# An unused 64-byte tile ahead of layer 0's pools in a two-layer hybrid attention / recurrence kernel

## The chip, the cores and the metric

The kernel runs on one core of one Trainium2 chip. The metric is the device time of one execution in microseconds; the median of several executions counts.

## The reference

The reference runs two layers over 1024 latent tokens and 256 context tokens of width 1024, in float32. Layer 0 projects the normalised tokens with one large matrix (9232 columns) into the parts of two mixers, 16 heads of neighbourhood attention and 4 heads of a bidirectional mLSTM, and projects their gated outputs back:

```python
qa, ka, va, za, qb, kb, vb, ob, zb, g = _split_cols(h @ w_in, AB_SIZES)
...
oa_l = _neighbourhood_attention(qa_l, ka_l, va_l, ka_c, va_c, rpb)
hb_l, hb_c = _mlstm_bidir(mb_l, mb_c, need_ctx)
...
return jnp.concatenate([ya, yb], axis=-1) @ w_out
```

Layer 1 has 16 heads of a bidirectional gated recurrence (HGRN2) between an input and an output projection of the same kind. Each layer's result is added to the stream with a gate per column.

## The kernel before

**Products.** TensorE takes float32 here in a rounded form, so each projection is made of three matmuls: an operand x is split into a rounded part (h) and the rest (l), and `dense` (lines 128 to 134) adds h times h, h times l and l times h for each of eight blocks of 128 rows:

```python
for k in range(nk):
    mm(ps, lhsT=lh(k), rhs=rh(k), start=(start and k == 0), stop=False, skip_group_check=skip)
    mm(ps, lhsT=lh(k), rhs=rl(k), start=False, stop=False, skip_group_check=skip)
    m = mm(ps, lhsT=ll(k), rhs=rh(k), start=False, stop=(stop and k == nk - 1), skip_group_check=skip)
```

These are the profile's lines L131, L132 and L133. `lhsT` is the stationary operand, which a weight load (PEld in the profile) brings into the array, and `rhs` the moving one, which streams through. The profile's rows name the moving operand first: `mm<-wh,hh` has the weights moving and the tokens stationary, `mm<-hh,wh` the other way round.

**The forms of layer 0.** `hh` and `hl` hold the split, normalised tokens (128 partitions, 8 blocks of 1280 tokens). `proj_nat` has 256 or 512 weight columns moving against 128 stationary tokens: 256 in `na_qk`, `na_values` and `proj_out`, 512 in `proj_wide`. `proj_tr` has 512 tokens moving (256 for the context) against 128 stationary weight columns, in `na_z` and `proj_out_tr`. The output projection (`out_sum`, lines L923 to L925) has 512 columns of the output weights moving against 128 stationary tokens of the mixers' result (`yh`, `yl`). Its weights lie in tiles `woh`, `wol`; six of eight blocks of its first half, `wh` and `wl`, still lie in layer 0's ring.

**Weights.** `wblock` (lines 81 to 121) fetches 128 x 512 weights by DMA into `wraw`, splits them on ScalarE and VectorE into `wh` and `wl`, and takes these tiles from a ring of six (`self.slabs`) in the pool `w0`.

**Stages of layer 0.** First the modulation, the normalisation and the first values (pool `pre`), then the gates of the mLSTM beside two more projections (pools `graw` and `gates`), then the attention of eight pairs of heads, with the next pair's projections and parts of the mLSTM's woven in (pool `na`), then the mLSTM's recurrence with the remaining projections woven in as filler (pool `ml`), then the output projection. A scheduler orders the instructions of each engine when the kernel is built.

**Where tiles lie.** Tiles are cut from each partition's bytes by pools that are stacked from the left, or, with `side="right"`, from the right end. On the left come the constants (pool `const`), then `mlk` (tables that the mLSTM keeps), `w0`, and above them in turn `graw`, `pre`, `gates`, `na` and `ml`. On the right lie `edge` (32 bytes), `hh` and `hl`, and later the output projection's tiles. At the end of layer 0 its pools are closed, and those of layer 1 begin again right behind `const`. The lines are these:

```python
edge = es.enter_context(tc.tile_pool(name="edge", bufs=1, side="right"))
...
self.open_h(right)
l0 = es.enter_context(ExitStack())
mlk = l0.enter_context(tc.tile_pool(name="mlk", bufs=1))
self.wp = l0.enter_context(tc.tile_pool(name="w0", bufs=2))
```

Of the kernel before, what the change touches and what calls it, by code (L numbers as in the profile page):

```python
# [10 lines left out]
F32 = mybir.dt.float32  # L11
# [8 lines left out]
P = 128  # L20
# [25 lines left out]
class Prog:  # L46
# [1520 lines left out]
    def build(self):  # L1567
        tc, nc, a = self.tc, self.nc, self.a
        dma = nc.sync.dma_start
        with ExitStack() as es:  # L1570
# [71 lines left out]
            self.open_h(right)  # L1642
            l0 = es.enter_context(ExitStack())
            mlk = l0.enter_context(tc.tile_pool(name="mlk", bufs=1))
            self.wp = l0.enter_context(tc.tile_pool(name="w0", bufs=2))
            self.rawp = self.wp
            self.slabs = 6
# [621 lines left out]
```

## Time and profile before

| | before |
|---|---|
| median of 3 runs | 3318.89 us (3318.3 to 3319.4) |
| the profiled execution | 3318.67 us |
| its span, first to last instruction | 3316.9 us |
| DMA queues | 286,032 packets, 236.73 MB by SyncE's; 51,760 packets, 138.94 MB by GpSimd's |
| granted TensorE clock | 9 or more tenths in all 40 slices |

How to read it: the page divides the span by engine, then by lines. A group's row gives line, engine, operation, tiles, shape and count, then the busy time of the group, the mean duration of one in ns, and the idle time ahead of it. The timeline gives start and duration in us of each instruction. A matmul's duration runs over its passage through the array, and several are under way at a time; how fast they follow each other is read from the spacing of their starts.

### The profile page before, as it was taken

What the parts mean: (1) busy time and instruction counts of PE and PEld (TensorE: products, weight loads), DVE (VectorE), ACT (ScalarE), POOL (GpSimd) and SP (SyncE); (2) the same over time, 40 slices, a digit from 0 to 9 for tenths busy, and PEclk for the clock granted to TensorE, in tenths of its full rate; (3) what the DMA queues carried; (4) which work ended last, traced back from release to release, by engine and by line L of the source; (5) the groups of instructions that cost most, each with busy time, mean ns of one, the idle gap of its engine ahead of it and who ended that gap; (6) DMA issues with size and microseconds to landing.
All of it is one profiled execution on the core that took longest, in us unless ns stands there. A gap on an engine that the chain in (4) does not pass through costs nothing.

```text
span 3316.9 us, 64819 instructions
## 1 busy us (share of the span) xinstructions
PE 3268.9 (99%) x24814; PEld 2905.1 (88%) x24814; DVE 2173.8 (66%) x4978; ACT 1455.9 (44%) x3396; POOL 796.5 (24%) x1191
## 2 busy tenths in 40 slices
PE   7999999999999999999999999999999999999999
PEld 6699899988989888898888788899999999999977
DVE  5337666666655566687767755577677677677756
ACT  5335554455544444455446333333433433433443
POOL 2222222222211112221110233312333333333110
PEclk9999999999999999999999999999999999999999
DMA  7713222232233433444653333322322324334376
GB/s 246 247 52 84 85 71 82 69 94 84 72 87 105 145 113 123 131 141 144 210 179 100 100 102 105 104 74 76 120 76 93 117 79 112 95 85 107 91 213 165
DMA packets 338102, 379.82 MB, mean 115 GB/s; under 512 B 34600, under 2 KB 269800, under 8 KB 336768
## 3 DMA queue, kind: packets, MB, share of 16 engines
q1 hardware_dynamic: 286032, 236.73, 24.2%
q0 software_dynamic: 51760, 138.94, 13.3%
q8 instruction: 196, 3.21, 0.4%
q14 instruction: 114, 0.93, 0.1%
HBM read 272.31 MB, written 103.08 MB: 113 GB/s over the span
## 4 chain that ended last, share of the span: by engine, by line
PE 80%; DVE 7%; issue 5%; DMA 4%; ACT 2%; POOL 1%; SPq 1%; DVEq 0%; POOLq 0%; ACTq 0%
PE mm L131 15%; PE mm L132 14%; PE mm L133 14%; PE acc L861 2%; PE s L1401 2%; PE tr L841 2%; PE mm L923 2%; PE mm L925 2%; PE mm L924 2%; PE x L131 2%; PE x L133 2%; PE x L132 2%; PE acc L633 2%; PE s L642 2%; PE s L1472 1%
## 5 line engine op out<-in xcount | busy, mean ns | idle before, releaser
L131 PE MATMUL mm<-wh,hh 128*128 128x256 f32 (+1 forms) x1440 | 446.2, 310 | 2.2 <-DVE graw L1694 0.8
L132 PE MATMUL mm<-wl,hh 128*128 128x256 f32 (+1 forms) x1440 | 444.9, 309 | 0.0
L133 PE MATMUL mm<-wh,hl 128*128 128x256 f32 (+1 forms) x1440 | 442.2, 307 | 0.0
L131 PE MATMUL mm<-hh,wh 128*128 128x512 f32 (+1 forms) x1076 | 392.0, 364 | 1.0 <-ACT p L1211 0.7
L132 PE MATMUL mm<-hl,wh 128*128 128x512 f32 (+1 forms) x1076 | 387.6, 360 | 0.7 <-DVE hl L318 0.7
L133 PE MATMUL mm<-hh,wl 128*128 128x512 f32 (+1 forms) x1076 | 387.4, 360 | 0.0
L131 PE MATMUL mm<-wzh,hh 128*128 128x256 f32 x1024 | 296.4, 289 | 0.0
L131 PEld LDWEIGHTS mm<-wh,hh 128*128 128x128 f32 x1440 | 271.6, 189 | 21.1 <-ACT ev L352 3.4
L132 PE MATMUL mm<-wzl,hh 128*128 128x256 f32 x1024 | 286.2, 280 | 0.0
L133 PE MATMUL mm<-wzh,hl 128*128 128x256 f32 x1024 | 285.6, 279 | 0.0
L132 PEld LDWEIGHTS mm<-wl,hh 128*128 128x128 f32 x1440 | 271.6, 189 | 12.3 <-issue 0.7
L133 PEld LDWEIGHTS mm<-wh,hl 128*128 128x128 f32 x1440 | 271.4, 189 | 12.0 <-issue 0.5
L131 PEld LDWEIGHTS mm<-hh,wh 128*128 128x128 f32 x1076 | 202.9, 189 | 33.5 <-ACT ev L371 4.2
L133 PEld LDWEIGHTS mm<-hh,wl 128*128 128x128 f32 x1076 | 202.6, 188 | 29.7 <-issue 0.2
L132 PEld LDWEIGHTS mm<-hl,wh 128*128 128x128 f32 x1076 | 202.9, 189 | 28.6 <-DVE hl L318 1.4
L131 PEld LDWEIGHTS mm<-wzh,hh 128*128 128x128 f32 x1024 | 192.8, 188 | 2.4
L132 PEld LDWEIGHTS mm<-wzl,hh 128*128 128x128 f32 x1024 | 192.7, 188 | 0.0
L133 PEld LDWEIGHTS mm<-wzh,hl 128*128 128x128 f32 x1024 | 192.0, 188 | 0.0
L74 DVE TENSOR_TENSOR wl<-wraw,wh 128x512 fp32r<-128x512 f32 x174 | 118.6, 689 | 85.6 <-ACT wh L73 83.8
L1436 ACT COPY gksel<-gK 128x1024 f32<-128x1024 f32 x96 | 110.9, 1155 | 100.1 <-DVE gK L1431 43.7
L1431 DVE TENSOR_TENSOR gQ<-gQ,gF 128x1024 f32<-128x1024 f32 x112 | 140.4, 1253 | 20.4 <-PE s L1401 20.4
L1431 DVE TENSOR_TENSOR gK<-gK,gF 128x1024 f32<-128x1024 f32 x112 | 140.2, 1251 | 18.8 <-ACT gksel L1436 11.4
(598 smaller groups left out, 8523.8 us busy)
## 6 DMA issues: line engine op xcount, KB each, us to landing
wraw<-in_wab_dram SPq DMA_DIRECT2D x108, 256.0 KB
wraw<-yd SPq DMA_DIRECT2D x92, 256.0 KB
br<-in_wc_dram SPq DMA_DIRECT2D x66, 256.0 KB
md<-ev POOLq DMA_DIRECT2D x60, 256.0 KB, 2.6
wraw<-in_wc_dram SPq DMA_DIRECT2D x120, 128.0 KB
mloz<-md SPq DMA_DIRECT2D x40, 256.0 KB
s<-gyt POOLq DMA_DIRECT2D x36, 256.0 KB, 5.7
adar<-in_wada_dram SPq DMA_DIRECT2D x16, 512.0 KB
```

The lines of the kernel that those rows point to most:

```text
L74: nc.vector.tensor_tensor(out=lo, in0=x, in1=hi.bitcast(F32), op=ALU.subtract)
L131: mm(ps, lhsT=lh(k), rhs=rh(k), start=(start and k == 0), stop=False, skip_group_check=skip)
L132: mm(ps, lhsT=lh(k), rhs=rl(k), start=False, stop=False, skip_group_check=skip)
L133: m = mm(ps, lhsT=ll(k), rhs=rh(k), start=False, stop=(stop and k == nk - 1), skip_group_check=skip)
L633: nc.tensor.matmul(num, lhsT=qc[:, j, :], rhs=C[d][:, j, :], start=False, stop=(j == 1))
L642: nc.tensor.matmul(u, lhsT=st["k"][c][:, j * P : (j + 1) * P], rhs=vw, start=True, stop=True)
L841: nc.tensor.transpose(pt[:nk, i, :], pr[:, o : o + nk], self.ident)
L861: m = nc.tensor.matmul(yp[h64], lhsT=v[:, h64], rhs=pTs[hd][:nk, i, :], start=(i == turn[0]), stop=(i == turn[-1]), tile_position=(0, hd * ...
L923: mm(ps, lhsT=yh[k], rhs=w.h(kk), start=(kk == 0), stop=False)
L924: mm(ps, lhsT=yh[k], rhs=w.l(kk), start=False, stop=False)
L1431: nc.vector.tensor_tensor(out=v, in0=v, in1=tot, op=ALU.mult)
L1436: m = nc.scalar.copy(ksel.rearrange("p (b s i) -> p b s i", s=2, i=h), pick(K))
```

## The change

A tile of 128 partitions by 16 float32 values, 64 bytes in each partition, is taken from the pool `mlk` before anything else is. Nothing writes or reads it.

```diff
             self.open_h(right)
             l0 = es.enter_context(ExitStack())
             mlk = l0.enter_context(tc.tile_pool(name="mlk", bufs=1))
+            self.t(mlk, [P, 16], F32, "pad", 1)
             self.wp = l0.enter_context(tc.tile_pool(name="w0", bufs=2))
             self.rawp = self.wp
             self.slabs = 6
```

The lists of instructions of all five engines hold the same instructions in the same order with the same waits as before; only the running numbers in the tiles' names and the line numbers behind the insertion (by one) differ. What differs otherwise is the start of each tile in the left-hand pools of layer 0: 64 bytes later in its partition. The starts, as the two programs give them, modulo 256 bytes:

| tiles | pool | before | after |
|---|---|---|---|
| `ident` (moving operand of the transposes) | const | 128 | 128 |
| `wh`, `wl`, `wraw`, `ev` of layer 0 | w0 | 128 | 192 |
| `wxh`, `wxl` of the first wide product | graw | 0 | 64 |
| `wxh`, `wxl` of the later wide products | ml | 128 | 192 |
| `hh`, `hl` of layer 0 | right | 192 | 192 |
| `woh`, `wol`, `yh`, `yl` of layer 0's output projection | right | 192 | 192 |
| layer 1: `hh`, `hl`, `wh`, `wl` | right | 192 | 192 |
| layer 1: `wzh`, `wzl` | left | 0 | 0 |

All steps within these tiles that a projection's matmul takes (blocks, tokens, weight columns) are multiples of 512 bytes, so each of its operands starts where its tile does, modulo 256. The first values, 272 columns wide, are the exception: their weights step by 1088 bytes.

## The prediction

> **What bounds the kernel now.** I read the page first, for the share of the engines and the chain that ended last, then the table of windows by stage, the list of waits, the groups of instructions by shape, and last the timeline of single matmuls, since this change can act only through how fast single instructions run.
>
> ```profile
> span 3316.9 us, 64819 instructions
> PE 3268.9 (99%) x24814; PEld 2905.1 (88%) x24814; DVE 2173.8 (66%) x4978; ACT 1455.9 (44%) x3396; POOL 796.5 (24%) x1191
> PE 80%; DVE 7%; issue 5%; DMA 4%; ACT 2%; POOL 1%; SPq 1%; DVEq 0%; POOLq 0%; ACTq 0%
> ```
>
> TensorE is busy in 99% of the span and carries 80% of the chain; VectorE carries 7%. The change touches layer 0 alone, so the table of windows is read there. Its columns after the length are busy time and count for PE, PEld, DVE, ACT and POOL, the granted clock, the DMA share and GB/s.
>
> ```profile
> 90.00:200.00 110.00, 110.00 (x634) 81.59 (x631) 32.80 (x82) 32.09 (x66) 25.68 (x45) 1.00 0.56 186
> 200.00:1090.00 890.00, 888.04 (x7098) 812.01 (x7097) 559.26 (x1761) 442.32 (x1191) 194.69 (x263) 1.00 0.28 80
> 1200.00:1620.00 420.00, 418.87 (x2282) 363.24 (x2281) 303.90 (x950) 206.15 (x533) 89.48 (x202) 1.00 0.43 131
> ```
>
> From 90 to 1620 us TensorE has a matmul in flight nearly all the time, at full clock. The list of waits of TensorE in the window 90:1620 has nine rows, of which these are the first and the last:
>
> ```profile
> PE acc L861 <- DVE apT L851: 1.1, 3, 0.4
> PE acc L633 <- DVE mqc L629: 0.2, 1, 0.2
> ```
>
> The nine come to 5.0 us in 1530. So in layer 0 nothing else is waited for: a matmul that takes 1 ns longer there moves the end by close to 1 ns.
>
> **The change part by part.** It adds no instruction, no DMA and no wait, and moves none. What it moves is places: all left-hand tiles of layer 0 start 64 bytes later in each partition, while the right-hand tiles (hh, hl and the output projection's tiles) stay. Every instruction of ScalarE, VectorE and GpSimd and every DMA is costed at nothing. What hides them is the 5.0 us of waits above, and VectorE shows no dependence on the place:
>
> ```profile
> L74 DVE TENSOR_TENSOR wl<-wraw,wh 128x512 fp32r<-128x512 f32 x142 | 96.5, 688 | 60.3 <-ACT wh L73 58.7
> L74 DVE TENSOR_TENSOR wl<-wraw,wh 128x512 fp32r<-128x512 f32 x32 | 22.1, 691 | 25.3 <-ACT wh L73 25.1
> ```
>
> The first row is layer 0 (window 0:1700), the second layer 1; raw and split weights start at other places there (0 and 192 in place of 128, all starts modulo 256), and the mean differs by 3 ns. If that cover were gone, 142 instructions of 3 ns would be 0.4 us, either way.
>
> What is left is TensorE, and here the timeline has a surprise. I call **distance** the start of the moving tile minus the start of the stationary one, modulo 256. The numbers of a row are start and duration; durations hold the pipeline's depth, so I use the spacing of the starts. First the 256-column products of layer 0 with weights moving and hh stationary, distance 128 - 192 = 192, in two undisturbed stretches:
>
> ```profile
> 191.00 0.28 PE L131 MATMUL mm<-wh,hh 128*128 128x256 f32 x1
> ...
> 204.49 0.28 PE L133 MATMUL mm<-wh,hl 128*128 128x256 f32 x1
> ...
> 228.74 0.28 PE L131 MATMUL mm<-wh,hh 128*128 128x256 f32 x1
> ...
> 237.33 0.28 PE L132 MATMUL mm<-wl,hh 128*128 128x256 f32 x1
> ```
>
> 119 steps in 13.49 us are 113.4 ns each; 73 steps in 8.59 us are 117.7. The same instruction settles at one of two spacings and stays there until something interrupts it. Over the start column of layer 0, 3,243 of these matmuls are followed at once by another projection matmul; 3,045 of those steps are free of a bubble (under 139 ns), 58% of them at 115 or less, mean 115.4. I take that mean, which lies between the two stretches.
>
> Next the same width with hh moving and weights stationary: layer 0, distance 192 - 128 = 64, 27 steps; then layer 1 at distance 192 - 192 = 0, 17 steps; then another place of layer 1 at distance 0, 35 steps:
>
> ```profile
> 944.64 0.28 PE L132 MATMUL mm<-hl,wh 128*128 128x256 f32 x1
> ...
> 947.82 0.28 PE L132 MATMUL mm<-hl,wh 128*128 128x256 f32 x1
> ...
> 2267.45 0.28 PE L131 MATMUL mm<-hh,wh 128*128 128x256 f32 x1
> ...
> 2269.48 0.28 PE L133 MATMUL mm<-hh,wl 128*128 128x256 f32 x1
> ...
> 1810.21 0.28 PE L131 MATMUL tr<-hh,st4h 128*128 128x256 f32 x1
> ...
> 1814.40 0.28 PE L133 MATMUL tr<-hh,wl 128*128 128x256 f32 x1
> ```
>
> 117.8, 119.4 and 119.7 ns. At distance 0 it settles near 120, above both spacings of distance 192, and it does so in two different parts of layer 1 (st4h, with which the second stretch begins, starts at 192 like the weights). Now 512 columns: layer 0 with hh moving, distance 64, 30 steps and 23 steps; layer 0 with weights moving, distance 192, 31 steps; then distance 0, layer 1 with hh moving (59 steps) and layer 0's output projection with weights moving (133 steps):
>
> ```profile
> 210.50 0.39 PE L131 MATMUL mm<-hh,wh 128*128 128x512 f32 x1
> ...
> 217.37 0.39 PE L131 MATMUL mm<-hh,wh 128*128 128x512 f32 x1
> ...
> 721.12 0.39 PE L132 MATMUL mm<-hl,wh 128*128 128x512 f32 x1
> ...
> 726.48 0.40 PE L131 MATMUL mm<-hh,wh 128*128 128x512 f32 x1
> ...
> 1123.75 0.39 PE L132 MATMUL mm<-wl,hh 128*128 128x512 f32 x1
> ...
> 1130.98 0.40 PE L133 MATMUL mm<-wh,hl 128*128 128x512 f32 x1
> ...
> 1787.89 0.40 PE L131 MATMUL mm<-hh,wh 128*128 128x512 f32 x1
> ...
> 1801.30 0.39 PE L133 MATMUL mm<-hh,st4l 128*128 128x512 f32 x1
> ...
> 1639.71 0.39 PE L924 MATMUL mm<-wol,yh 128*128 128x512 f32 x1
> ...
> 1669.86 0.40 PE L925 MATMUL mm<-woh,yl 128*128 128x512 f32 x1
> ```
>
> 229.0, 233.0, 233.2, 227.3 and 226.7 ns. At this width distance 0 is the best of all, with either operand moving. The pad brings nearly every projection of layer 0 to distance 0: weights to 192, hh already there. So the 256-column products lose and the 512-column products gain. The counts in layer 0, from the groups by shape in the window 0:1700, one of three equal lines each:
>
> ```profile
> L131 PE MATMUL mm<-wh,hh 128*128 128x256 f32 x1200 | 345.7, 288 | 0.9 <-ACT ev L389 0.6 <-ACT ev L720 0.3
> L131 PE MATMUL mm<-hh,wh 128*128 128x512 f32 x384 | 152.2, 396 | 0.0
> L132 PE MATMUL mm<-wl,hh 128*128 128x512 f32 x240 | 99.6, 415 | 0.0
> L131 PE MATMUL mm<-hh,wh 128*128 128x256 f32 x192 | 54.2, 282 | 0.0
> ```
>
> Steps that count are those followed by another projection matmul; means are over the start column, free of bubbles, as above:
>
> - 256 columns, weights moving, distance 192 to 0: 115.4 to 119.3 (a little under 119.7, as bursts begin lower), 3.9 ns x 3,243 = **+12.6 us**. Bounds: 117.7, the slow spacing of today, gives +7.5; 120 gives +14.9; the fast one, 113.4, gives -6.5.
> - 256 columns, hh moving, 64 to 0: 117.3 to 119.3, 2.0 x 526 = **+1.1**. Bounds 0 and +1.3.
> - 512 columns, hh moving, 64 to 0: mean 230.1 to 228.0 (the mean of all 2,580 clean steps at distance 0 is 227.9), -2.1 x 1,065 = **-2.2**. Bounds: 226.7 gives -3.6, no change gives 0.
> - 512 columns, weights moving, 192 to 0 (the wide products, and the tail rows L923 to L925 that still use the left ring): mean 233.2 to 228.2 (those bursts begin anew more often), -5.0 x 913 = **-4.6**. Bounds: 226.7 gives -5.9, 230.1 gives -2.8.
> - The first wide product's two extra tiles go from distance 64 to 128: +2.6 ns x 49 = +0.1.
>
> Transposes with ident moving change distance as well, the largest group being
>
> ```profile
> L841 PE MATMUL tr<-ident,aP 128*128 128x128 f32 x480 | 85.0, 277 | 0.0
> ```
>
> I take 0 for them; 1 ns either way on these 480 is 0.5 us, and on all such groups about 1.
>
> The sum is +12.6 + 1.1 - 2.2 - 4.6 + 0.1 = +7.0 us. On the profiled execution's own time, 3318.67 us (span 3316.9 and 1.8 around it), this is 3325.7; the median of the three runs is 3318.89, 0.2 above it. I predict **3326 us**, +0.21%.
>
> [...] The rows above show 113.4, 117.7, 119.4 and 119.7 ns for one shape. [...]
>
> **The rivals.**
>
> 1. *The place does not matter.* The two spacings at distance 192 show that one place can give both, so what looks like distance may be how bursts begin. Against it: at 512 columns three stretches at 64 and 192 lie at 229 to 233 and two at 0, with opposite operands moving, at 227. Then all terms are 0: 3318.7, no change.
> 2. *Faster: the 256-column products settle low at distance 0.* No row shows weights moving at distance 0 at this width, both rows that I use have hh moving. If such bursts fall into a low state like that of 191 us, the first term is -6.5 in place of +12.6 and the rest is -5.6: 3306.6. If they only stay at 115.4, the sum is -5.6: 3313.1. The point from which it decides is a mean of 115.4 + 5.6 / 3.243 = 117.1 ns: below it the change pays, above it costs. For it speaks that bursts in layer 0 are often broken by attention work and so begin anew; against it, that both contexts at distance 0 reach 119 to 120 within a dozen steps.
>
> **How the numbers follow.** Forecast 0.64, no effect 0.19, faster 0.17. A measurement of this kernel tells 0.2%, 6.6 us, from no change: the limits are 3312.3 and 3325.5. Around 3326 the bounds of the terms leave about 7 in 10 of the forecast's chance above 3325.5, and 3 in 10 within. Of the faster case three quarters lie under 3312.3. So slower 0.45, same 0.19 + 0.19 + 0.04 = 0.42, faster 0.13. The range: upwards the first term's bound of +14.9 with 2.5 from the others gives 3331; downwards it must take in the no-effect case and the mild form of the faster one, 3313, and I end it at 3312.
>
> **What would show it.** Right: the 256-column stretches with weights moving at 119 to 120 ns and no second spacing near 113; the wide 512-column stretches near 227 to 228; the time lost between 200 and 1090 us (+7 or more, the projections for q, k, o and z), 1 or 2 us won back in 90 to 200 and 1200 to 1620, layer 1's spacings unchanged. Wrong in the first term: 113 or 117 ns there. Wrong altogether: all spacings as today, or a new wait in the list for TensorE, which would mean that a DMA or another engine minds its new place.

## The result, and the profile after

The changed kernel takes **3329.78 us** (median of 9 runs, 3325.95 to 3331.36) against 3318.89 us for the kernel before on the same chip (9 runs, 3317.10 to 3321.41). The ratio is **1.0030, 95% interval 1.0020 to 1.0041**: slower by 0.3%, 3.8 us above the forecast of 3326 and 1.2 us inside the upper end of its range. The profiled execution took 3331.36 us; it is the slowest of the nine. One of the eight executions of e9, below, took 16,850 us, five times the others, and is not in its ratio.

The first lines of the page of the changed kernel:

```profile
span 3329.6 us, 64819 instructions
PE 3283.6 (99%) x24814; PEld 2922.1 (88%) x24814; DVE 2171.8 (65%) x4978; ACT 1457.5 (44%) x3396; POOL 797.5 (24%) x1191
PE 79%; DVE 7%; issue 5%; DMA 5%; ACT 2%; POOL 1%; SPq 1%; DVEq 0%; POOLq 0%; ACTq 0%
```

The counts are those of before, and TensorE alone is busier: 14.7 us more in a span that is 12.7 us longer. VectorE, ScalarE and GpSimd stay within 2.0 us. The table of windows by stage, and the first row and the last of TensorE's list of waits in the window 90:1620:

```profile
90.00:200.00 110.00, 110.00 (x631) 81.55 (x624) 32.87 (x82) 32.08 (x66) 25.01 (x46) 1.00 0.57 188
200.00:1090.00 890.00, 888.24 (x7009) 813.79 (x7009) 555.07 (x1744) 440.20 (x1184) 194.15 (x262) 1.00 0.28 80
...
PE acc L861 <- DVE apT L851: 0.9, 3, 0.4
...
PE mm L131 <- ACT ev L720: 0.2, 1, 0.2
```

Between 200 and 1090 us TensorE is as busy as before (888 of 890 us, full clock) but starts 7009 matmuls in place of 7098. The list of waits has eight rows, 4.6 us in all, against nine and 5.0: no new wait. So each matmul takes longer, and the timeline shows which. These are the same matmuls as the prediction's six stretches of layer 0 whose distance changes, found by their order in the program, which is the same in both kernels:

```profile
191.31 0.28 PE L131 MATMUL mm<-wh,hh 128*128 128x256 f32 x1
205.59 0.28 PE L133 MATMUL mm<-wh,hl 128*128 128x256 f32 x1
...
230.21 0.28 PE L131 MATMUL mm<-wh,hh 128*128 128x256 f32 x1
238.96 0.28 PE L132 MATMUL mm<-wl,hh 128*128 128x256 f32 x1
...
952.60 0.28 PE L132 MATMUL mm<-hl,wh 128*128 128x256 f32 x1
955.84 0.28 PE L132 MATMUL mm<-hl,wh 128*128 128x256 f32 x1
...
211.90 0.40 PE L131 MATMUL mm<-hh,wh 128*128 128x512 f32 x1
218.73 0.39 PE L131 MATMUL mm<-hh,wh 128*128 128x512 f32 x1
...
727.65 0.40 PE L132 MATMUL mm<-hl,wh 128*128 128x512 f32 x1
732.88 0.39 PE L131 MATMUL mm<-hh,wh 128*128 128x512 f32 x1
...
1133.80 0.40 PE L132 MATMUL mm<-wl,hh 128*128 128x512 f32 x1
1140.87 0.39 PE L133 MATMUL mm<-wh,hl 128*128 128x512 f32 x1
```

With 119, 73, 27, 30, 23 and 31 steps the spacings are 120.0, 119.9, 120.0, 227.7, 227.4 and 228.1 ns; before they were 113.4, 117.7, 117.8, 229.0, 233.0 and 233.2. The two speeds of the first two stretches have become one, above both.

Since both records hold all 24,814 matmuls in the same order, each step (from one start to the next) can be set beside its twin. The sums over layer 0, with the mean of the steps that are free of a bubble in both:

| products | distance | steps | mean before, after (ns) | sum (us) | forecast (us) |
|---|---|---|---|---|---|
| 256 columns, weights moving | 192 to 0 | 3,230 | 115.4, 119.5 | +11.9 | +12.6 |
| 256 columns, hh moving | 64 to 0 | 533 | 117.3, 119.4 | +1.1 | +1.1 |
| 512 columns, hh moving | 64 to 0 | 1,088 | 230.1, 229.0 | -1.3 | -2.2 |
| 512 columns, weights moving | 192 to 0 | 913 | 233.2, 229.5 | -2.9 | -4.6 |
| the two wx tiles | 64 to 128 | 49 | 229.2, 231.9 | +0.1 | +0.1 |
| everything else in layer 0 | | | | +2.5 | 0 |
| layer 1 | | | | +2.1 | 0 |

A count by the prediction's rule (any projection matmul may follow) gives 3,243, 526 and 1,061 steps in the first three rows, and +12.0, +1.1 and -1.2 us. The whole, 13.5, less 0.9 us by which the first matmul starts earlier, is the 12.7 between the spans. By stage of before it is +0.5 us from 90 to 200, +9.3 from 200 to 1090, -0.4 up to 1200, and 0.0 from 1200 to 1620.

### The profile page after: what moved, and what is told of

Same layout as the page of the kernel before. It is cut to its first block, busy times and chain, and to the rows that moved or that the text cites. A ratio compares the mean times of both kernels' runs of the same rounds, so it can differ in the third digit from the quotient of the medians.

```text
span 3329.6 us, 64819 instructions
## 1 busy us (share of the span) xinstructions
PE 3283.6 (99%) x24814; PEld 2922.1 (88%) x24814; DVE 2171.8 (65%) x4978; ACT 1457.5 (44%) x3396; POOL 797.5 (24%) x1191
## 4 chain that ended last, share of the span: by engine, by line
PE 79%; DVE 7%; issue 5%; DMA 5%; ACT 2%; POOL 1%; SPq 1%; DVEq 0%; POOLq 0%; ACTq 0%
PE mm L131 15%; PE mm L132 14%; PE mm L133 14%; PE acc L861 2%; PE s L1401 2%; PE tr L841 2%; PE mm L923 2%; PE mm L925 2%; PE mm L924 2%; PE x L131 2%; PE x L132 2%; PE x L133 2%; PE acc L633 2%; PE s L642 2%; PE s L1472 1%
## 5 line engine op out<-in xcount | busy, mean ns | idle before, releaser
L132 PEld LDWEIGHTS mm<-wl,hh 128*128 128x128 f32 x1440 | 273.9, 190 | 11.9 <-issue 0.7
L74 DVE TENSOR_TENSOR wl<-wraw,wh 128x512 fp32r<-128x512 f32 x174 | 118.7, 690 | 83.8 <-ACT wh L73 79.3
L1431 DVE TENSOR_TENSOR gK<-gK,gF 128x1024 f32<-128x1024 f32 x112 | 139.7, 1247 | 18.8 <-ACT gksel L1436 11.4
```

The lines of the kernel that those rows point to most:

```text
L74: nc.vector.tensor_tensor(out=lo, in0=x, in1=hi.bitcast(F32), op=ALU.subtract)
L1431: nc.vector.tensor_tensor(out=v, in0=v, in1=tot, op=ALU.mult)
```

## The experiments

In all of them the matmuls keep the order that they had before, but for 14 of them in e8, and each is set against executions of the kernel before on the same chip. The theories: **A**, the spacing depends on the distance between moving and stationary tile; **B**, it depends on where the left-hand tiles start; **C**, each new layout costs something by chance. Diffs are against the kernel before.

**e1: only hh and hl move.** The same distance is reached from the other side.

```diff
             self.open_h(right)
+            self.t(self.hpool, [P, 16], F32, "hpad", 1)
```

> Without the pad on the left; an unused 64-byte tile behind hl in layer 0's right-hand pool moves hh and hl alone, from 192 to 128 modulo 256, and no other tile. Weights stay at 128, so distance is 0 as in the changed kernel. Theory A (distance between moving and stationary tile): same cost as the change, about 3329 us (3326 to 3332); 256-column products with weights moving at 119.5 ns, wide 512-column ones at 229.5, hh moving at 512 columns 229.0. Theory B (the weights', or another left-hand tile's, own start counts): as before, 3319; 115.4 and 233 ns. Theory C (any new layout costs something by chance): neither set of spacings.

Measured: 3329.10 us against 3320.40 (23 runs of before, shared by e1 to e4), ratio 1.0028 (1.0017 to 1.0039). The stretch that took 113.4 ns before, on the timeline of e1:

```profile
191.81 0.28 PE L131 MATMUL mm<-wh,hh 128*128 128x256 f32 x1
206.09 0.28 PE L133 MATMUL mm<-wh,hl 128*128 128x256 f32 x1
```

119 steps of 120.0 ns. Over layer 0 the four forms of the table stand at 119.6, 119.4, 228.9 and 229.3 ns, those of the changed kernel within 0.3. Here two tiles have moved, and the weights, the attention tiles and every target of a DMA have not. B falls.

**e2: both sides move, the distance stays.**

```diff
-            self.t(cp, [P, 16], F32, "pad")
...
             self.open_h(right)
+            self.t(self.hpool, [P, 16], F32, "hpad", 1)
...
             lk = self.fp = l1.enter_context(tc.tile_pool(name="hgk", bufs=1))
+            self.t(lk, [P, 16], F32, "pad", 1)
```

> Weights and all left-hand tiles of layer 0 move down by 64 bytes (the unused tile among the constants is left out, and put back ahead of layer 1), and hh and hl move down by 64 too: weights at 64, hh at 128, distance 192 as before the change although every large tile of layer 0 has moved. Theory A: 3319 us (3317 to 3321); 115.4 ns at 256 columns with weights moving, 233 at 512. Theory B: not as before, since the weights' start is new; a cost like the change's, 3326 or more. Theory C: a time of its own.

Measured: 3318.98 us, ratio 0.9997 (0.9988 to 1.0005). The first two stretches of e2:

```profile
190.85 0.28 PE L131 MATMUL mm<-wh,hh 128*128 128x256 f32 x1
204.34 0.28 PE L133 MATMUL mm<-wh,hl 128*128 128x256 f32 x1
...
228.59 0.28 PE L131 MATMUL mm<-wh,hh 128*128 128x256 f32 x1
236.86 0.28 PE L132 MATMUL mm<-wl,hh 128*128 128x256 f32 x1
```

113.4 and 113.3 ns; the means over layer 0 are 115.5, 116.8, 230.1 and 233.1, as before. The weights and both halves of the activations have moved and nothing is lost, so C falls too. And the second stretch, at 117.7 ns in the kernel before, is at 113.3 here: which of the two speeds a burst takes at distance 192 is not fixed by the distance. Nor is it a matter of chance in each execution: in e7 and e8 below, whose layer 0 lies as in the kernel before, 98 of 100 bursts of at least 12 steps take the same speed as there, in e2 83. What decides it stays open.

**e3 and e4: distances 64 and 128.** e3 has a pad of 128 bytes, e4 moves the left-hand tiles down by 64 (e2 without its hpad line).

```diff
             mlk = l0.enter_context(tc.tile_pool(name="mlk", bufs=1))
+            self.t(mlk, [P, 32], F32, "pad", 1)
```

> The pad of the change is 128 bytes in place of 64: weights at 0, hh at 192, distance 64 with weights moving and 192 with hh moving. Theory A gives each form the spacing that layer 1 has at these places: weights moving, 256 columns 117.2 ns (+1.8 x 3,243 = +6.0 us over before), hh moving 256 columns 113.8 (-3.5 x 526 = -1.8), hh moving 512 columns 233.2 (+3.1 x 1,065 = +3.3), weights moving 512 columns 229.8 (-3.4 x 913 = -3.1): 3323 us (3320 to 3326). Theory B with a cost that grows with the shift: above 3330. Theory C: a time of its own.

> Only the left-hand tiles of layer 0 move down by 64: weights at 64, hh at 192, distance 128 either way. Theory A: 512 columns at 232.6 ns, as layer 1 shows at 128 (hh moving +2.5 x 1,065 = +2.7 us, weights moving -0.6 x 913 = -0.5); for 256 columns no row shows 128: between 113.4 and 119.7 ns the first term is -6.5 to +13.9 us and the second -2.0 to +1.3, so 3313 to 3336, and all steps of one form move together. Theory B: as e2, since the left-hand tiles stand at the same places.

Measured: e3 3325.31 us, ratio 1.0013 (1.0005 to 1.0022); e4 3331.05, ratio 1.0033 (1.0021 to 1.0046). First e3 (the 119 steps with weights moving, the 27 with hh moving), then e4 (the 119):

```profile
191.32 0.28 PE L131 MATMUL mm<-wh,hh 128*128 128x256 f32 x1
205.33 0.28 PE L133 MATMUL mm<-wh,hl 128*128 128x256 f32 x1
...
950.12 0.28 PE L132 MATMUL mm<-hl,wh 128*128 128x256 f32 x1
953.19 0.28 PE L132 MATMUL mm<-hl,wh 128*128 128x256 f32 x1
```

```profile
192.53 0.28 PE L131 MATMUL mm<-wh,hh 128*128 128x256 f32 x1
206.65 0.28 PE L133 MATMUL mm<-wh,hl 128*128 128x256 f32 x1
```

117.7 and 113.7 ns, then 118.7. In e3 hh moving has taken the low speed that the weights had, and the weights the speed that hh had: what counts is moving minus stationary, not which of the two is a weight. The low speed is not gone at distance 64: 14 of 100 bursts with weights moving still take it, against 74 of the same 100 at 192. Twice the shift costs half as much as the change, which no cost that grows with the shift gives. The four terms of e3 are +5.5, -0.9, +3.2 and -2.6 us against the expected +6.0, -1.8, +3.3 and -3.1. In e4 the 512-column products stand at 232.6 and 232.5 ns, as expected for distance 128. Its left-hand tiles lie where they lie in e2, and it is 12 us slower than e2, which B does not allow.

**e5: the same distance from 256 bytes below.** The left-hand tiles move down by 192.

```diff
-            self.t(cp, [P, 16], F32, "pad")
...
-            sg = self.t(cp, [P, KD, 2], F32, "sct")
+            sg = self.ab[1][:, 0, :, :].rearrange("p v k -> p k v")
...
-            mx = self.t(cp, [P, 16], F32, "lbm")
+            mx = self.ab[1][:, 1, :, :].rearrange("p v k -> p (v k)")
...
             lk = self.fp = l1.enter_context(tc.tile_pool(name="hgk", bufs=1))
+            self.t(lk, [P, 48], F32, "pad", 1)
```

> All left-hand tiles of layer 0 move down by 192 bytes (three small tiles among the constants are left out or laid over a tile that is free then; 192 bytes are put back ahead of layer 1). Weights start at 192 modulo 256 as in the changed kernel, 256 bytes below it; distance 0. Theory A with a period of 256: as the changed kernel, 3329 us (3326 to 3332), 119.5 ns at 256 columns with weights moving. If the period is longer than 256 bytes (512, say): other spacings than 119.5 and 229, and another time.

Measured: 3329.34 us against 3320.92 (27 runs, shared by e5 to e8), ratio 1.0028 (1.0019 to 1.0036). The 119 steps of e5 again:

```profile
190.76 0.28 PE L131 MATMUL mm<-wh,hh 128*128 128x256 f32 x1
205.04 0.28 PE L133 MATMUL mm<-wh,hl 128*128 128x256 f32 x1
```

120.0 ns; the four forms stand at 119.5, 119.4, 229.0 and 229.6, within 0.1 of the changed kernel's 119.5, 119.4, 229.0 and 229.5. Here places 256 bytes apart act alike.

**e6: a pad of 32 bytes.**

```diff
             mlk = l0.enter_context(tc.tile_pool(name="mlk", bufs=1))
+            self.t(mlk, [P, 8], F32, "pad", 1)
```

> The pad is 32 bytes: distance 224 with weights moving, 32 with hh moving, which no projection row of 256 or 512 columns has. Theory A: a spacing of its own for each form, steady over layer 0. The 272-column products of layer 0 stand at 32, 96, 160 and 224 and take 124.8 to 125.7 ns at all four, 117.4 to 118.3 for 256 columns by the column: +2.0 to +2.9 ns x 3,243 = +6.5 to +9.4 us, the other three forms between -8 and +4: 3326 us (3318 to 3333). Theory C (chance): spacings that change from stretch to stretch.

Measured: 3331.97 us, ratio 1.0032 (1.0020 to 1.0044), inside the expected range but 6 us above its middle. The 119 steps take 118.3 ns:

```profile
192.38 0.28 PE L131 MATMUL mm<-wh,hh 128*128 128x256 f32 x1
206.46 0.28 PE L133 MATMUL mm<-wh,hl 128*128 128x256 f32 x1
```

At 512 columns nothing is won: 233.3 ns with hh moving (distance 32) and 232.9 with weights moving (224). So half a step of 64 loses the low speed of the one width and finds none for the other.

**e7 and e8: the rule used in layer 1.** There wz stood at 0 and hh at 192, distance 64, which e3 shows is not the best for 256 columns. e7 is the last pair of lines alone, e8 both.

```diff
                 sp, s1 = [lo.enter_context(tc.tile_pool(name=n, bufs=1, reuse_waits="tile")) for n in ("st", "s1")]
+                self.t(sp, [P, 48], F32, "pads", 1)
...
-                        ("hgb", ()),
+                        ("hgb", (("padz", 1, 32),)),
```

> Layer 0 as before the change. In layer 1 an unused 128-byte tile moves the 256-column weights wz from 0 to 128, hh stays at 192: distance 64 to 192 with weights moving (2,959 steps), 192 to 64 with hh moving (384). Theory A: 117.2 ns falls to between 113.8 and 115.4 (-5.4 to -10.1 us), 113.8 rises to 117.3 (+1.3): 4 to 9 us faster than before, 3314 us (3311 to 3317). Rival: layer 1 is bound by VectorE, ScalarE or a wait, or the rule holds in layer 0 alone: within 2 us of before.

> As the kernel with wz moved by 128 bytes, and layer 1's st tiles moved by 192 too, so that their 512-column products (576 steps, moving st, stationary weights) go from distance 64 to 0: 229.8 to between 227.3 and 228.1 ns, -1.0 to -1.4 us. Theory A: 3313 us, about 1 us below the kernel with wz alone. Rival as there.

Measured: e7 **3315.50 us**, ratio 0.9982 (0.9972 to 0.9991); e8 **3314.80**, ratio 0.9979 (0.9971 to 0.9988). Both beat the kernel before and the changed one. A stretch of 46 steps in layer 1, first in the kernel before, then in e7:

```profile
3072.92 0.28 PE L132 MATMUL mm<-wzl,hh 128*128 128x256 f32 x1
3078.34 0.28 PE L133 MATMUL mm<-wzh,hl 128*128 128x256 f32 x1
```

```profile
3068.54 0.28 PE L132 MATMUL mm<-wzl,hh 128*128 128x256 f32 x1
3073.77 0.28 PE L133 MATMUL mm<-wzh,hl 128*128 128x256 f32 x1
```

117.8 and 113.7 ns. Over layer 1 the 2,959 steps with wz moving go from 117.2 to 114.2 ns, -8.8 us, and the 368 with hh moving from 113.8 to 117.8, +1.4: -7.4 together, of which 5.4 show between the medians. The 512-column products of the st tiles, 35 steps, before and in e8:

```profile
2066.24 0.40 PE L131 MATMUL x<-st2h,wh 128*128 128x512 f32 x1
2074.27 0.39 PE L133 MATMUL x<-st3h,wl 128*128 128x512 f32 x1
```

```profile
2067.39 0.39 PE L131 MATMUL x<-st2h,wh 128*128 128x512 f32 x1
2075.32 0.39 PE L133 MATMUL x<-st3h,wl 128*128 128x512 f32 x1
```

229.4 and 226.6 ns, -1.6 us over 576 steps. The times of e7 and e8 differ by less than their intervals; the spacings show the second gain, the times do not.

**e9: hh moves, hl stays.** Which stationary tile counts, the one in use or the next, which is loaded meanwhile? (In the first stretch of before the matmul at 191.00 us takes 0.28 us, and the weight load for the one that follows it at 191.11 runs from 191.00 for 0.19.)

```diff
-    def open_h(self, es):
+    def open_h(self, es, pad=0):
...
         self.hh = self.t(self.hpool, [P, KD, T], F32R, "hh", 1)
+        pad and self.t(self.hpool, [P, pad], F32, "hpad", 1)
...
-            self.open_h(right)
+            self.open_h(right, 16)
```

> As the kernel before, but of the two halves of the activations hh alone moves down by 64 bytes (192 to 128); hl stays at 192, weights at 128. The products run in threes (wh on hh, wl on hh, wh on hl), so with weights moving the distance to the stationary tile in use is 0, 0, 192, and to the next one, which is loaded meanwhile, 0, 192, 0. Theory A1 (the tile being loaded counts): 256-column spacings 119.5, 115.4, 119.5 ns in this order. Theory A2 (the tile in use counts): 119.5, 119.5, 115.4. Theory A3 (a state that a burst falls into): all three alike, between 115.4 and 119.5. In each case about two thirds of the change's cost in layer 0: 3326 us (3323 to 3328).

Measured: 3329.28 us against 3319.83, ratio 1.0028 (1.0017 to 1.0039), above the 3323 to 3328 that all three theories gave. The two stretches of e9:

```profile
191.13 0.28 PE L131 MATMUL mm<-wh,hh 128*128 128x256 f32 x1
205.15 0.28 PE L133 MATMUL mm<-wh,hl 128*128 128x256 f32 x1
...
229.76 0.28 PE L131 MATMUL mm<-wh,hh 128*128 128x256 f32 x1
238.36 0.28 PE L132 MATMUL mm<-wl,hh 128*128 128x256 f32 x1
```

Both 117.8 ns. By product, in the order of the three, layer 0 gives 118.1, 117.7 and 118.2 ns with weights moving. Neither A1 nor A2 shows at this width; A3 is nearest, a burst has one speed. With weights moving at 512 columns the order of A2 does show: the wide products stand at 230.5, 230.2 and 232.7 ns, twice near the 229.5 of distance 0 and then near the 233.2 of 192. With hh moving the tile in use doesn't settle it, nor does an average: the three are at 231.4 to 232.8 ns, above both the 230.1 of distance 64 and the 229.0 of distance 0 of which they are mixed. Why the speed depends on the distance stays open.

## Why the prediction was right, and where it was not

*The path.* TensorE bounds layer 0, nothing else is late, and the other engines and the DMAs cost nothing: shown by the unchanged counts, by the list of waits (4.6 us in 1530), and by e1, where the left-hand tiles stay and the time is the same (3329.10 us, and 3329.78 with the change).

*The first term, right.* 119.5 ns measured, 119.3 forecast; all 104 bursts of at least 12 such steps lie between 119 and 121 ns after their first six, where before 77 lay under 115 and 26 between 116.5 and 118.2. The faster rival needed a mean under 117.1 and is gone. The no-effect rival is refuted by e1 against e2 (119.6 and 115.5 ns). The four forms together cost 8.8 us net (11.9 + 1.1 - 1.3 - 2.9). Why the place of a tile changes the spacing, no run here shows.

*The gains at 512 columns, right in sign, too large.* The step at fault is "2.1 ns" and "5.0 ns" better: I took 228.0 and 228.2 ns from the mean of all steps at distance 0, which come mostly from long bursts in layer 1 and the output projection. Layer 0's bursts are short, and at distance 0 a burst begins slowly: in the wide products the first six steps now average about 231 ns, the next six 228 and the six after that 227, and over half of their steps are among the first six. At distance 192 all of them, the first six too, stood near 233. Measured: 1.1 and 3.6 ns better, inside the bounds given, so 2.6 us of the forecast 6.8 did not come.

*The stages.* "+7 or more" between 200 and 1090 us came (+9.3). "1 or 2 us won back" in 90 to 200 and 1200 to 1620 did not (+0.5 and 0.0): I had counted only the wide products there. Of 256-column steps with weights moving 149 and 505 lie in these stages, and their +0.9 and +0.9 us eat the -0.5 and -1.5 of the wide ones.

*The rest of layer 0, +2.5 us, not forecast.* 1.2 of it falls before 90 us, mostly bubbles around the 272-column products, whose own spacing is unchanged (125.2 ns); 0.8 is bubbles in the output projection; 0.3 are the last steps of 47 bursts, behind which the attention's scores follow (114.3 to 119.9 ns). In e1 and e5, at the same distance, all of layer 0 comes to +9.7 and +9.9 us in place of +11.4, so one or two of these 2.5 belong to the execution and not to the change. The products with ident, costed at 0 to 1 us, came to -0.7.

*Layer 1.* Its spacings are unchanged, as forecast (2,959 steps at 117.2 ns in both). Its +2.1 us are the balance of waits and of the clock, at which the prediction did not look. One wait ahead of L1472 takes 1.8 us more than before. ScalarE's copy of gkn (L1414), which ends it, starts behind a cast of new weights, and that cast waited for its DMA, first in the kernel before, then in the changed one:

```profile
2963.13 0.62 ACT L73 CAST wzh<-wraw 128x512 fp32r<-128x512 f32 x1 [4.78 <-DMA wraw<-in_wc_dram]
```

```profile
2977.09 0.62 ACT L73 CAST wzh<-wraw 128x512 fp32r<-128x512 f32 x1 [6.67 <-DMA wraw<-in_wc_dram]
2978.25 0.60 PE L1472 MATMUL s<-gv,gkn 128*128 128x128 f32 x3 [1.66 <-ACT gkn L1414]
```

From the matmul ahead of it to this one pass 2.05 us, and 0.23 in the record of before. It does not go by the distance: in e1 to e9 this step takes 1.8, 2.0, 2.0, 1.6, 0.4, 2.2, 0.8, 2.3 and 2.1 us. And there are three stretches in which TensorE had half its clock. The table of windows of the changed kernel, each of the three behind the window of equal length ahead of it:

```profile
1845.94:1849.36 3.42, 1.71 (x7) 0.94 (x6) 3.42 (x7) 1.62 (x4) 0.00 (x0) 1.00 0.06 16
1849.36:1852.77 3.41, 3.41 (x10) 2.64 (x9) 3.39 (x7) 1.25 (x3) 0.54 (x1) 0.50 0.42 140
1856.18:1859.59 3.41, 1.48 (x7) 0.88 (x5) 2.83 (x5) 0.62 (x1) 0.78 (x2) 1.00 0.61 191
1859.59:1863.00 3.41, 3.36 (x8) 2.68 (x9) 1.76 (x3) 1.26 (x2) 1.09 (x2) 0.50 0.48 155
3224.93:3228.34 3.41, 1.50 (x6) 0.65 (x5) 2.23 (x4) 2.71 (x5) 0.00 (x0) 1.00 1.08 369
3228.34:3231.75 3.41, 3.41 (x9) 2.67 (x10) 2.92 (x5) 1.82 (x4) 0.00 (x0) 0.50 1.05 382
```

Granted clock 0.50 for 3.41 us with TensorE busy, each time behind 3.41 us in which it was busy for half or less (1.71, 1.48, 1.50). Each sets TensorE back by 1.5 us against before. The second keeps it; behind the first and the third, waits are shorter by as much, or more, so that from 3180 us to the end 1.3 us are won in all. These three, +1.8, +1.5 and -1.3, make the +2.1 to within 0.1. Apart from the one at its very end, the profiled execution of before has no such stretch, and those of e1 to e9 have 1, 2, 2, 0, 1, 1, 1, 3 and 1, whatever their distance. In each record the stretches begin at whole multiples of 3.413 us from one another (the first and the third here lie 404 of them apart). Cut into windows on that grid from 60 us on, every stretch at half clock follows a window with TensorE busy for 51% or less, and every busier window is followed by full clock; three between 48 and 51% were spared. In the kernel before TensorE has the same short waits there, but on its grid (placed by the stretch at its end) the three emptiest windows ahead of that end are busy for about 59 to 64%, two of them the first and the third row here:

```profile
1834.00:1837.40 3.40, 2.17 (x9) 1.21 (x7) 3.40 (x7) 2.15 (x4) 0.00 (x0) 1.00 0.01 2
1837.40:1840.80 3.40, 2.91 (x13) 2.39 (x14) 3.33 (x6) 1.24 (x2) 0.54 (x1) 1.00 0.28 77
1840.90:1844.30 3.40, 2.10 (x10) 1.42 (x9) 3.40 (x7) 1.90 (x4) 0.00 (x0) 1.00 0.20 77
1844.30:1847.70 3.40, 2.79 (x12) 1.94 (x11) 2.86 (x6) 0.62 (x1) 1.07 (x2) 1.00 0.34 116
```

So in these records whether a wait of 1.7 us costs up to another 1.5 goes by where the grid falls in the execution, not by the pad. Of the 23 runs of before beside e1 to e4, eight had a mean clock of 1.000 and averaged 3319.1 us, fourteen had 0.999 and averaged 3320.9. The forecast's sum was made on an execution with none of these and with the short wait at L1472, 3318.67, up to 2 us below the medians of the kernel before (3318.9, 3320.4, 3320.9 and 3319.8). With the spacings as measured it would give 3318.7 + 8.9 (the 8.8 and the 0.1 of the wx tiles) = 3327.6, so 2.2 us of the changed kernel's median lie in parts that were costed at nothing, and that the range held them is in part luck.

## What to carry to other kernels

Where TensorE is busy in 99% of the span, with float32 products as here (no other type was run), the place of its operands is worth trying as a tuning parameter: set moving start minus stationary start, modulo 256 bytes (weights 256 bytes lower, in e5, gave the same spacings), by an unused tile ahead of one of them. In this kernel 256-column products were fastest at 192 (115.4 and 115.6 ns) and slowest at 0 (119.5 and 119.4), 512-column ones fastest at 0 (229.5 and 229.0) and slowest at 192 and 32 (233.1 to 233.3); look which shape holds the time, and keep the two halves of a split operand at one place (apart, in e9, the 512-column products with hh moving took 231.4 to 232.8 ns). Read it from the starts of consecutive matmuls in a long burst, not from their durations (0.28 us at a spacing of 113.4 ns and of 120.0), and beware of any edit of a pool that shifts tiles in passing: here it cost 0.3% or won 0.2% with no instruction changed.

## What the runs showed of the hardware that was not expected

- The dependence itself, with the best and the worst distance, 192 and 0, exchanged between the widths. Means over layer 0, free of bubbles, with weights moving and with hh moving (0 from the changed kernel, 128 from e4, 32 and 224 from e6, 64 and 192 from before and e3):

| distance | 256 columns (ns) | 512 columns (ns) |
|---|---|---|
| 0 | 119.5, 119.4 | 229.5, 229.0 |
| 32 | -, 117.3 | -, 233.3 |
| 64 | 117.3, 117.3 | 229.7, 230.1 |
| 128 | 118.7, 118.7 | 232.5, 232.6 |
| 192 | 115.4, 115.6 | 233.2, 233.1 |
| 224 | 118.3, - | 232.9, - |

- Two speeds for one instruction at one distance (113.4 and 117.7 ns at 192 and at 64), chosen by burst: the low one in 74 of 100 bursts at 192, in 14 at 64, in none at 0. The same layout repeats the choice (98 of 100 bursts in e7 and in e8); the burst at 228.74 us took the upper speed before and the lower one in e2.
- Operands at mixed distances do not simply average: in e9 the 512-column products with hh moving are slower (231.4 to 232.8 ns) than at either of the two distances (230.1 and 229.0), while those with weights moving go by the distance of the tile in use (230.5, 230.2 and 232.7 ns for 0, 0 and 192).
- Half clock for 3.41 us behind a window of 3.41 us in which TensorE was busy for 31 to 51% (three windows of 48 to 51% were spared), on a grid whose place changes from execution to execution (counted from the start of the span, the grids of before and of the changed kernel lie 1.7 us apart).
